# Another order of the seven products over two column blocks of the feed-forward input

## The chip, the cores and the metric

The kernel runs on one core of a Trainium2 chip, in one launch. The time is the device time of that launch in microseconds; a comparison takes runs of both kernels on the same chip. Besides the times there is one execution with the hardware profiler on, from which all rows below come.

## What is computed

Two layers of an encoder on 512 tokens of width 1024. Each layer has a mixing part (four kinds of heads, an output projection) and a feed-forward part; only the latter is touched. Cut to that part, the reference reads:

```python
h = rmsnorm(x, ffn_norm_pre[l])
gate, up = jnp.split(h @ ffn_w_in[l], 2, axis=-1)      # 2 x 2816 columns
f = (jax.nn.silu(gate) * up) @ ffn_w_out[l]
x = x + rmsnorm(f, ffn_norm_post[l])
```

The 2816 columns of `gate` and of `up` are 22 blocks of 128 each (`KF`).

## The kernel before

Every matrix is held as two float32r parts, a high one and the remainder, and a product of two matrices is three matmuls (high by high, high by low, low by high), issued by `mm3`. ScalarE makes the high part with a copy that the profile calls CAST, VectorE the low part with a subtraction (TENSOR_TENSOR into a `wl` or `m` tile).

In the feed-forward input the first three blocks (`NP`) of each layer are multiplied plainly. For the blocks 3 to 21, here called pairs (gate and up of one block over two halves of the rows of h, 256 tokens each, and two halves of the inner dimension), the 2 by 2 block product is formed with seven products in place of eight. A product is 12 matmuls of 256 columns over four tiles of 128 (`prod`, L1466) and adds into one half of a PSUM bank. Each pair has two banks: `bd`, with the halves u0 and g1, and `bx`, with g0 and u1. Products and halves: 1 into g0; 5 into u1; 6, 7 and 4 into u0; 3 into g1; 2 into g0.

Between the products the other engines work on the same two banks (`pair_side`, L1480):

- after 1: ScalarE copies g0 (in bx) to u0 (in bd). The profile calls it COPY bd<-bx.
- after 5: ScalarE copies u1 out of bx, COPY m<-bx.
- after 6: VectorE adds that copy to u0 and writes g1 (TENSOR_TENSOR bd<-bd,m).
- after 7: VectorE adds it to u0 again, into SBUF; this is the up half u1 (TENSOR_TENSOR m<-bd,m).
- after 2 and after 3: ScalarE's Silu of g0 and of g1 (ACTIVATE m<-bx, m<-bd); after 3 and after 4: VectorE's products of gate and up.

`ffn_in` (L1528) issues the products of two neighbouring pairs interleaved: of the new pair, and of the old one before it. The list of tuples at L1549 sets the order; the last entry of a tuple names a piece of the side work that must have been issued before.

The program has no order written out by hand for the whole. `go` (L350) runs generators ("threads") against modelled clocks and issues, each time, the instruction that it believes can start first; a `yield "P"`, `"A"`, `"V"`, `"G"`, `"D"` gives up the turn until an instruction of TensorE, ScalarE, VectorE, GpSimd or a transfer is due. `prod` yields once per two of its four tiles, so that a product can be issued in two halves of six matmuls. What is issued runs in that order on each engine. Where two engines touch one PSUM bank, the built program has a semaphore wait between them, whichever half of the bank each uses.

The weights of a pair are four tiles, of which two are formed by sums: `pair_load` (L466) loads a, e, c, b, d with SyncE and adds into e and c with GpSimd's accumulating transfers (L513); `form` (L546) splits one of them into the two parts, in the order of the consumption, which `i`, the running number of a weight, enforces; `sums` (L521) makes a2 = a + e and b2 = b + a2 on VectorE. In the numbers of the products: a is for 1, e for 5, a2 for 6, b for 2, c for 7, d for 4, b2 for 3. `w_load` (L441) hands out the numbers. Tiles come from a pool of 74 (`m`) and from four pairs of `wh` and `wl`.

Of the kernel before, what the change touches and what calls it, by code (L numbers as in the profile page):

```python
# [11 lines left out]
AF = mybir.ActivationFunctionType  # L12
# [4 lines left out]
L = 512  # L17
# [4 lines left out]
KF = FF // P  # L22
# [6 lines left out]
NP = 3  # L29
# [10 lines left out]
HALF = 256  # L40
# [196 lines left out]
class Builder:  # L237
# [203 lines left out]
    def w_load(self):  # L441
        n = 0
        for src, kind in self.stream():
            if kind == "pair":
                yield from self.pair_load(*src, n)
                n += 7 if src[1] > NP else 5
                n += 2 if src[1] == KF - 1 else 0
                continue
            yield lambda: self.tok["s"] or len(self.tok["m"]) >= 2 + STAGE
            k = "s" if self.tok["s"] else "m"  # L450
            self.take(k, 1 if k == "s" else 2)
            yield "D"
            if k == "s":
                st = self.wsp.tile([P, 1024], F32, tag="ws", name=self.nm("ws"))
                self.dma(st, src, 524288)
                half = [st[:, h * 512:(h + 1) * 512] for h in range(2)]
            else:
                half = [self.m(), self.m()]
                for h in range(2):
                    self.dma(half[h], src[:, h * 512:(h + 1) * 512], 262144)  # L460
            for h in range(2):
                self.spawn(self.w_split(n + h, half[h], kind, "" if k == "s" and h == 0 else k),
                           1 if n > 5 else n // 2 - 2.5)
            n += 2

    def pair_load(self, l, i, n):  # L466


        w = self.d["wf1"]
        src = {"a": w[l, i, 0][:, 0:512], "b": w[l, i, 0][:, 512:1024], "c": w[l, i, 1][:, 0:512],  # L470
               "d": w[l, i, 1][:, 512:1024]}
        q = {"n": set()}
        self.pairs[l, i] = q
        prev = self.pairs.get((l, i - 1))
        yield lambda: l in self.room_ok and i - self.pnow < 4
        order = (("a", "a", None), ("e", "c", "d"), ("c", "a", "c"), ("b", "b", None), ("d", "d", None))
        if SUMS == "V":
            order = (("a", "a", None), ("c", "c", None), ("d", "d", None), ("b", "b", None), ("e", None, None))

        late = i > NP  # L480
        at = dict(zip(("a", "e", "a2", "b", "c"), (n, n + 1, n + 2 + late, n + 3 + 2 * late, n + 4 + 2 * late)))
        for x in ("a", "e"):
            self.spawn(self.form(at[x], q, x), 1)
        if late:
            self.spawn(self.form(n + 2, prev, "d"), 1)
        self.spawn(self.form(at["a2"], q, "a2"), 1)
        if late:
            self.spawn(self.form(n + 4, prev, "b2"), 1)
        for x in ("b", "c"):
            self.spawn(self.form(at[x], q, x), 1)  # L490
        if i == KF - 1:
            for j, x in enumerate(("d", "b2")):
                self.spawn(self.form(n + 7 + j, q, x), 1)
        self.spawn(self.sums(q), 1)
        for name, first, more in order:
            yield lambda: len(self.tok["m"]) >= 1 + ROOM
            self.take("m", 1)
            q[name] = self.m()
            if first:
                self.spawn(self.part_load(q, name, src[first], src[more] if more else None), 0)  # L500
# [976 lines left out]
                     skip_group_check=True)  # L1477
        self.give(*w[2:])

    def pair_side(self, b, q, f, i):  # L1480

        u0, g1, g0, u1 = b[0][:, 0:HALF], b[0][:, HALF:L], b[1][:, 0:HALF], b[1][:, HALF:L]
        yield lambda: 1 in q
        yield "A"
        self.act.copy(u0, g0)
        q.add("u0")
        yield from self.need(2, 0)
        e, a = self.m(), self.m()
        yield lambda: 5 in q
        yield "A"  # L1490
        self.act.copy(e[:, 0:HALF], u1)
        yield lambda: 6 in q
        yield "V"
        self.dve.tensor_tensor(g1, u0, e[:, 0:HALF], ALU.add)
        q.add("g1")
        yield lambda: 7 in q
        yield "V"
        self.dve.tensor_tensor(e[:, HALF:L], u0, e[:, 0:HALF], ALU.add)
        q.add("u1")
        yield lambda: 2 in q  # L1500
        yield "A:Silu"
        self.act.activation(a[:, 0:HALF], g0, AF.Silu)
        self.give("x")
        yield lambda: 3 in q
        yield "A:Silu"
        self.act.activation(a[:, HALF:L], g1, AF.Silu)
        yield "V"
        self.dve.tensor_tensor(a[:, HALF:L], a[:, HALF:L], e[:, HALF:L], ALU.mult)
        self.give("m")
        yield lambda: 4 in q  # L1510
        yield "V"
        self.dve.tensor_tensor(a[:, 0:HALF], a[:, 0:HALF], u0, ALU.mult)
        self.give("d")
        self.spawn(self.f_conv(i, a, f), 4)
# [13 lines left out]
    def ffn_in(self, l, h, ok, f):  # L1528
        def done(i, b):
            if i % 2:  # L1530
                self.spawn(self.ffn_act(i // 2, b[i - 1:i + 1], f), 2)

        hf = {}
        self.conv, self.pnow = False, NP
        self.spawn(self.h_forms(l, h, ok, hf), 2)
        yield from self.parts(h, ok, "dx" * NP, CUTS, done)
        yield lambda: all((n, 3) in hf for n in (4, 7))
        self.give("m", 4)
        old = None
        for i in range(NP, KF + 1):  # L1540
            new = None
            if i < KF:
                self.pnow = i
                b = []
                for n in "dx":
                    b.append((yield from self.acq(n)))
                new = (b[1][:, 0:HALF], b[0][:, HALF:L], b[0][:, 0:HALF], b[1][:, HALF:L], set())
                self.spawn(self.pair_side(b, new[4], f, i), 0)
            for who, n, at, wait in ((new, 1, 0, 0), (new, 5, 3, 0), (old, 4, 2, "u1"), (new, 6, 2, "u0"),  # L1549
                                     (old, 3, 1, "g1"), (new, 2, 0, 0), (new, 7, 2, "g1")):  # L1550
                if who:
                    if wait:
                        yield lambda: wait in who[4]
                    yield from self.prod(who[at], n, hf, n == 1)
                    who[4].add(n)
            old = new
        self.conv = True
        self.give("m", 28)
# [153 lines left out]
```

## Time and profile before

| | us |
|---|---|
| median of 3 runs (1276.7 to 1277.62) | 1277.46 |
| profiled execution, its own time | 1276.97 |
| its span, first to last instruction | 1275.2 |
| TensorE busy in the span | 1225.8 (96%) |
| VectorE busy | 787.8 (62%) |
| ScalarE busy | 657.4 (52%) |
| pairs of layer 0, about | 309 to 514 |
| pairs of layer 1, about | 940 to 1146 |

The span is what the page divides; 1.8 us of the profiled execution lie around it. Busy TensorE is not TensorE at its peak, since matmuls overlap; the starts of the matmuls tell the pace.

### The profile page before, as it was taken

The page shows a single profiled execution, that of the slowest core. Times are in us where ns is not written, and L with a number is a line of the kernel's source. Part 1 is how long each engine was busy: PE and PEld are TensorE (multiplying, and loading weights), DVE is VectorE, ACT ScalarE, POOL GpSimd, SP SyncE. Part 2 cuts the span into 40 slices and gives each one's busy share as a digit, 9 for nine tenths or more (in the row PEclk, how much of TensorE's full clock was granted, in tenths as well). Part 3 has the DMA queues.
Part 4 walks back from the last instruction along what each step waited for, and adds up shares of the span by engine and source line. Part 5 has one row for each costly group of instructions (what it writes and reads, how often), then busy time and mean ns, then how long its engine had stood idle before and what let it go on. Part 6 is the DMA issues. An engine that isn't in the chain of part 4 may idle for free.

```text
span 1275.2 us, 21195 instructions
## 1 busy us (share of the span) xinstructions
PE 1225.8 (96%) x7906; PEld 1068.0 (84%) x7906; DVE 787.8 (62%) x1602; ACT 657.4 (52%) x1448; POOL 227.1 (18%) x216
## 2 busy tenths in 40 slices
PE   7999999999999999999999899999999999999997
PEld 7876777789999999888887676778899999998886
DVE  6477665589666777612555767655886667766222
ACT  6476744665444555523548656554654445545230
POOL 5021111241111110202230111112311111102120
PEclk9999999999999999999999899999999999999999
DMA  6532224127667552325451221250566665513331
GB/s 222 182 99 84 67 72 169 42 83 184 157 173 176 141 139 83 100 99 165 146 198 50 67 84 43 100 189 1 124 172 168 180 168 133 135 58 123 108 116 67
DMA packets 77239, 155.11 MB, mean 122 GB/s; under 512 B 9040, under 2 KB 9424, under 8 KB 77136
## 3 DMA queue, kind: packets, MB, share of 16 engines
q1 hardware_dynamic: 65904, 133.31, 32.1%
q0 software_dynamic: 10944, 19.93, 9.5%
q8 instruction: 62, 1.02, 0.3%
q10 hardware_dynamic: 288, 0.52, 0.2%
q14 instruction: 41, 0.34, 0.1%
HBM read 147.44 MB, written 4.19 MB: 119 GB/s over the span
## 4 chain that ended last, share of the span: by engine, by line
PE 83%; ACT 6%; DVE 6%; issue 2%; POOL 1%; DMA 1%; SPq 0%; DVEq 0%; POOLq 0%; ACTq 0%
PE bx L191 42%; PE bd L191 41%; DVE m L191 5%; ACT m L191 4%; ACT bd L191 1%; POOL s L191 1%; ACT L191 1%; ACT wh L191 1%; DVE s L191 1%; DMA ws<-in_w 0%; POOL wl L191 0%; DMA m<-in_w 0%; PE warm L191 0%; DVE wl L191 0%; POOL m L191 0%
## 5 line engine op out<-in xcount | busy, mean ns | idle before, releaser
L191 PE MATMUL bd<-m,wh 128*128 128x256 f32 (+1 forms) x1648 | 364.6, 316 | 1.3 <-ACT wh L191 1.2
L191 DVE TENSOR_TENSOR wl<-m,wh 128x512 fp32r<-128x512 f32 x284 | 197.1, 694 | 179.6 <-ACT wh L191 162.8
L191 ACT CAST wh<-m 128x512 fp32r<-128x512 f32 x316 | 195.8, 619 | 191.6 <-PE bd L191 112.8
L191 PEld LDWEIGHTS bd<-m,wh 128*128 128x128 f32 x1648 | 267.2, 191 | 22.7 <-issue 6.0
L191 PE MATMUL bx<-m,m 128*128 128x256 f32 (+8 forms) x1688 | 249.3, 337 | 11.3 <-DVE m L191 9.0
L191 PE MATMUL bd<-m,wl 128*128 128x256 f32 (+1 forms) x824 | 257.5, 313 | 0.0
L191 PEld LDWEIGHTS bx<-m,m 128*128 128x128 f32 (+3 forms) x1688 | 188.9, 177 | 61.8 <-issue 26.4
L191 DVE TENSOR_TENSOR m<-m,m 128x512 f32<-128x512 f32 (+3 forms) x288 | 172.2, 623 | 26.2 <-ACT m L191 23.8
L191 PE MATMUL bx<-m,wh 128*128 128x256 f32 x864 | 163.3, 287 | 15.2 <-ACT bd L191 15.2
L191 PEld LDWEIGHTS bd<-m,wl 128*128 128x128 f32 x824 | 157.1, 191 | 9.4
L191 PE MATMUL bx<-wh,m 128*128 128x512 f32 x472 | 163.5, 392 | 0.0
L191 PEld LDWEIGHTS bx<-m,wh 128*128 128x128 f32 x864 | 134.1, 191 | 22.1 <-ACT bd L191 22.1
L191 PE MATMUL bd<-wh,m 128*128 128x512 f32 x360 | 128.8, 392 | 0.0
L513 POOL DMA_DIRECT2D m<-in_wf x76 | 66.6, 936 | 336.9 <-DMA m<-in_wf 130.7
L191 PE MATMUL bx<-m,wl 128*128 128x256 f32 x432 | 122.0, 282 | 0.0
L191 ACT CAST wh<-ws 128x512 fp32r<-128x512 f32 x86 | 53.2, 621 | 126.7 <-PE bd L191 77.6
L191 DVE TENSOR_TENSOR wl<-ws,wh 128x512 fp32r<-128x512 f32 x56 | 40.6, 726 | 122.3 <-ACT wh L191 122.1
L191 PEld LDWEIGHTS bx<-wh,m 128*128 128x128 f32 x472 | 89.1, 189 | 19.0 <-issue 0.5
L191 PE MATMUL bd<-m,m 128*128 128x256 f32 (+1 forms) x696 | 101.9, 300 | 0.0
L191 POOL TENSOR_TENSOR wl<-m,wh 128x512 fp32r<-128x512 f32 x32 | 48.6, 1518 | 289.3 <-ACT wh L191 231.8
L191 PEld LDWEIGHTS bd<-m,m 128*128 128x128 f32 x696 | 93.9, 194 | 3.7
L191 PE MATMUL bx<-wl,m 128*128 128x512 f32 x236 | 92.2, 391 | 0.0
(105 smaller groups left out, 1443.5 us busy)
## 6 DMA issues: line engine op xcount, KB each, us to landing
m<-in_wf SPq DMA_DIRECT2D x234, 256.0 KB, 3.5
m<-in_wf POOLq DMA_DIRECT2D x76, 256.0 KB, 4.9
ws<-in_wf SPq DMA_DIRECT2D x34, 512.0 KB, 3.7
m<-in_w SPq DMA_DIRECT2D x64, 256.0 KB, 4.4
ws<-in_w SPq DMA_DIRECT2D x16, 512.0 KB, 3.8
m<-in_wo SPq DMA_DIRECT2D x24, 256.0 KB, 4.0
m<-in_x SPq DMA_DIRECT2D x14, 256.0 KB, 3.5
m<-in_rpb SPq DMA_DIRECT2D x12, 256.0 KB, 5.2
```

Source lines behind the costliest of these rows:

```text
L191: return f(out, *a, **k)
L513: self.nc.gpsimd.dma_start(q[name], src, accum_op=ALU.add)
```

## The change

Three places are edited. The list in `ffn_in` now interleaves the products as 1 (new), 7 (old), 5 (new), 3 (old), 6 (new), 2 (new), 4 (old), where it was 1, 5 (new), 4 (old), 6 (new), 3 (old), 2, 7 (new). The side work of a pair, one generator before, is two: `pair_first` with the two copies and the Silu of g0, and `pair_sums` with the rest; they meet in `q["e"]` and `q["s0"]`. And the numbers of the weights in `w_load` and `pair_load` follow the new order, so that c, b2 and d of a pair are formed one pair later.

```diff
@@ pair_load
-        late = i > NP
-        at = dict(zip(("a", "e", "a2", "b", "c"), (n, n + 1, n + 2 + late, n + 3 + 2 * late, n + 4 + 2 * late)))
...
+        use = [(q, "a"), (prev, "c"), (q, "e"), (prev, "b2"), (q, "a2"), (q, "b"), (prev, "d")]
+        if not late:
+            use = [u for u in use if u[0] is q]
         if i == KF - 1:
...
+            use += [(q, "c"), (q, "b2"), (q, "d")]
+        for j, (o, x) in enumerate(use):
+            self.spawn(self.form(n + j, o, x), 1)
@@ pair_side, now pair_first and pair_sums
-    def pair_side(self, b, q, f, i):
+    def pair_first(self, b, q, t):
...
         yield "A"
         self.act.copy(u0, g0)
         q.add("u0")
         yield from self.need(2, 0)
-        e, a = self.m(), self.m()
+        e, a = t["e"], t["a"] = self.m(), self.m()
         yield lambda: 5 in q
         yield "A"
         self.act.copy(e[:, 0:HALF], u1)
+        q.add("e")
...
+    def pair_sums(self, b, q, t, f, i):
...
+        yield lambda: 6 in q and "e" in q
@@ ffn_in
-            for who, n, at, wait in ((new, 1, 0, 0), (new, 5, 3, 0), (old, 4, 2, "u1"), (new, 6, 2, "u0"),
-                                     (old, 3, 1, "g1"), (new, 2, 0, 0), (new, 7, 2, "g1")):
+            for who, n, at, wait in ((new, 1, 0, 0), (old, 7, 2, "g1"), (new, 5, 3, 0), (old, 3, 1, "g1"),
+                                     (new, 6, 2, "u0"), (new, 2, 0, 0), (old, 4, 2, "u1")):
```

**TensorE, from product 1 to product 5 of one pair.** In these rows `bx` and `bd` are the banks (the number is that of a pair's tile), the first operand is a part of h, the second a part of the weight. Before, in layer 0, the end of product 1 and most of product 5:

```order
L191 MATMUL bx_4635<-m_2484,wh_4582 128x256 x2
L191 MATMUL bx_4635<-m_2484,wl_4583 128x256
L191 MATMUL bx_4635<-m_3285,wh_4598 128x256 [waits Activation_49]
L191 MATMUL bx_4635<-m_3285,wh_4598 128x256
L191 MATMUL bx_4635<-m_3285,wl_4599 128x256 [waits DVE_49]
L191 MATMUL bx_4635<-m_3287,wh_4598 128x256 x2
L191 MATMUL bx_4635<-m_3287,wl_4599 128x256
L191 MATMUL bx_4635<-m_3392,wh_4598 128x256 [waits Activation_49]
L191 MATMUL bx_4635<-m_3392,wh_4598 128x256
L191 MATMUL bx_4635<-m_3392,wl_4599 128x256
```

The same place in the change: first the end of product 1 and the start of product 7 of the old pair, then its end and the start of product 5 of the new one:

```order
L191 MATMUL bx_4757<-m_2484,wh_4703 128x256 x2
L191 MATMUL bx_4757<-m_2484,wl_4704 128x256
L191 MATMUL bd_4618<-m_3311,wh_4721 128x256 [waits DVE_49,Activation_49]
L191 MATMUL bd_4618<-m_3311,wh_4721 128x256
L191 MATMUL bd_4618<-m_3311,wl_4722 128x256 [waits DVE_49]
```

```order
L191 MATMUL bd_4618<-m_3541,wh_4721 128x256 x2
L191 MATMUL bd_4618<-m_3541,wl_4722 128x256
L191 MATMUL bx_4757<-m_3285,wh_4739 128x256 [waits Activation_49]
L191 MATMUL bx_4757<-m_3285,wh_4739 128x256
L191 MATMUL bx_4757<-m_3285,wl_4740 128x256 [waits DVE_49]
```

Before, product 5 followed product 1 into the same bank, six of its matmuls were issued ahead of the copy of g0, and the seventh waits for ScalarE. Now the 12 matmuls of product 7 into another bank stand between, and product 5 waits at its first matmul.

**VectorE, around the add of u1 after product 7** (`m` from `bd` and `m`). Before, then now:

```order
L191 TENSOR_TENSOR wl_4875<-m_4503,wh_4874 128x512 [waits PE_49,Activation_49]
L191 TENSOR_TENSOR m_4674<-m_4674,bd_4634 128x256
L191 TENSOR_TENSOR wl_4893<-m_4431,wh_4892 128x512 [waits DMAHW3_49,PE_49,Activation_49]
L191 TENSOR_TENSOR m_4810<-bd_4772,m_4810 128x256 [waits PE_49]
L191 TENSOR_TENSOR wl_4915<-m_4502,wh_4914 128x512 [waits Activation_49]
```

```order
L191 TENSOR_TENSOR wl_4878<-m_4483,wh_4877 128x512 [waits PE_49,Activation_49]
L191 TENSOR_TENSOR m_4657<-m_4657,bd_4618 128x256 [waits PE_49]
L191 TENSOR_TENSOR wl_4898<-m_4351,wh_4897 128x512 [waits Activation_49]
L191 TENSOR_TENSOR wl_4918<-m_4482,wh_4917 128x512 [waits PE_49,Activation_49]
L191 TENSOR_TENSOR m_4793<-bd_4756,m_4793 128x256 [waits PE_49]
```

The add now has the low part of a2 (`wl_4918`) ahead of it. On ScalarE, from the copy of g0 to the Silu of g1, the order before and now is:

```order
L191 COPY bd_4772<-bx_4773 128x256 [waits PE_49]
L191 CAST wh_4798<-m_4233 128x512 [waits Activation_49]
L191 COPY m_4810<-bx_4773 128x256 [waits DVE_49,PE_49]
L191 CAST wh_4819<-m_4380 128x512 [waits DMAHW2_49,DVE_49]
L191 CAST wh_4836<-m_4369 128x512 [waits DMASW3_49,DVE_49,PE_49]
L191 CAST wh_4855<-m_4502 128x512 [waits DMAHW4_49,DVE_49,PE_49]
L191 ACTIVATE m_4674<-bd_4634 128x256 [waits PE_49]
```

```order
L191 COPY bd_4756<-bx_4757 128x256 [waits PE_49]
L191 CAST wh_4780<-m_4348 128x512 [waits DVE_49,Activation_49]
L191 CAST wh_4802<-m_4351 128x512 [waits DMAHW2_49,DVE_49,PE_49]
L191 COPY m_4793<-bx_4757 128x256 [waits PE_49]
L191 CAST wh_4819<-m_4249 128x512 [waits DMAHW6_49,DVE_49]
L191 ACTIVATE m_4657<-bd_4618 128x256 [waits DVE_49,PE_49]
```

One CAST stands between the two copies before, two now; the Silu of g1 now waits for VectorE as well (for the add of u1, which reads the same bank).

**TensorE, the last pair of a layer, which no new pair follows.** Before, the end of product 7 and the start of product 4; then the change, from the middle of product 3 to that of product 4:

```order
L191 MATMUL bd_5994<-m_3541,wh_6037 128x256 x2
L191 MATMUL bd_5994<-m_3541,wl_6038 128x256
L191 MATMUL bd_5994<-m_3332,wh_6055 128x256 [waits DVE_49,Activation_49]
L191 MATMUL bd_5994<-m_3332,wh_6055 128x256
L191 MATMUL bd_5994<-m_3332,wl_6056 128x256
```

```order
L191 MATMUL bd_5978<-m_2489,wl_6056 128x256
L191 MATMUL bd_5978<-m_2491,wh_6055 128x256 [waits DVE_49]
L191 MATMUL bd_5978<-m_2491,wh_6055 128x256
L191 MATMUL bd_5978<-m_2491,wl_6056 128x256
L191 MATMUL bd_5978<-m_2493,wh_6055 128x256 x2
L191 MATMUL bd_5978<-m_2493,wl_6056 128x256
L191 MATMUL bd_5978<-m_3332,m_6067 128x256 [waits Activation_49]
L191 MATMUL bd_5978<-m_3332,m_6067 128x256
L191 MATMUL bd_5978<-m_3332,m_6068 128x256
L191 MATMUL bd_5978<-m_3334,m_6067 128x256 x2
L191 MATMUL bd_5978<-m_3334,m_6068 128x256
L191 MATMUL bd_5978<-m_3447,m_6067 128x256 [waits Activation_49]
```

Before, the products 4 and 3 stood behind the last 7 and only the first of them waited for VectorE. Now 7, 3 and 4 of the last pair stand one behind the other in one bank, 3 waits in its middle for VectorE (the add of u1) and 4 in its middle for ScalarE (the Silu of g1).

## Rows read from the trace of the kernel before

**Rows 1.** The page: busy time by engine, and the chain that ended last.

```profile
PE 1225.8 (96%) x7906; PEld 1068.0 (84%) x7906; DVE 787.8 (62%) x1602; ACT 657.4 (52%) x1448; POOL 227.1 (18%) x216
...
PE 83%; ACT 6%; DVE 6%; issue 2%; POOL 1%; DMA 1%; SPq 0%; DVEq 0%; POOLq 0%; ACTq 0%
```

**Rows 2.** Waits of TensorE: total us, times, longest; whole span, then 309 to 514.

```profile
PE bx L191 <- ACT bd L191: 16.9, 38, 0.4
...
PE bx L191 <- ACT bd L191: 8.5, 19, 0.4
```

**Rows 3.** Chain of waits in one pair of layer 0: start, us, what.

```profile
471.24 2.17 PE bx L191 x18
...
473.43 0.37 ACT bd L191
...
473.84 0.98 PE bx L191 x6
474.82 4.32 PE bd L191 x36
479.14 1.44 PE bx L191 x12
480.58 1.44 PE bd L191 x12
482.02 2.17 PE bx L191 x18
```

**Rows 4.** Timeline behind the next pair's start, on TensorE, ScalarE and VectorE.

```profile
483.89 0.28 PE L191 MATMUL bx<-m,wl 128*128 128x256 f32 x1
484.21 0.36 ACT L191 COPY bd<-bx 128x256 f32<-128x256 f32 x1 [1.32 <-PE bx L191]
484.48 0.62 ACT L191 CAST wh<-m 128x512 fp32r<-128x512 f32 x1
484.62 0.50 PE L191 MATMUL bx<-m,wh 128*128 128x256 f32 x2 [0.45 <-ACT bd L191]
...
484.96 0.28 PE L191 MATMUL bx<-m,wl 128*128 128x256 f32 x1
...
485.13 0.69 DVE L191 TENSOR_TENSOR wl<-m,wh 128x512 fp32r<-128x512 f32 x1 [1.81 <-ACT wh L191]
```

**Rows 5.** Windows, the pairs of layer 0 in two stretches (engines' busy us, clock, DMA share, GB/s).

```profile
323.36:410.00 86.64, 83.07 (x678) 81.46 (x677) 55.99 (x99) 41.03 (x85) 13.87 (x16) 1.00 0.70 173
410.00:513.00 103.00, 98.99 (x809) 97.16 (x808) 73.21 (x126) 52.24 (x106) 10.36 (x12) 1.00 0.45 116
```

**Rows 6.** Chain of waits at the first pair of layer 0, between products 1 and 5.

```profile
314.61 0.37 ACT bd L191
```

**Rows 7.** Groups by form, 323.7 to 506.96: busy us, mean ns; idle before, released by.

```profile
L191 DVE TENSOR_TENSOR wl<-m,wh 128x512 fp32r<-128x512 f32 x102 | 70.5, 691 | 44.7 <-ACT wh L191 40.3
L191 ACT CAST wh<-m 128x512 fp32r<-128x512 f32 x102 | 63.2, 620 | 41.1 <-PE bd L191 32.3 <-PE bx L191 4.7 <-ACT m L191 2.1
...
L191 DVE TENSOR_TENSOR m<-bd,m 128x256 f32<-128x256 f32 x17 | 7.2, 424 | 4.0 <-PE bd L191 4.0
...
L191 ACT ACTIVATE m<-bd 128x256 f32<-128x256 f32 x17 | 6.5, 384 | 17.2 <-PE bd L191 17.2
```

**Rows 8.** Transfers of the feed-forward weights by queue: count, KB, us to landing.

```profile
m<-in_wf SPq DMA_DIRECT2D x234, 256.0 KB, 3.5
m<-in_wf POOLq DMA_DIRECT2D x76, 256.0 KB, 4.9
```

**Rows 9.** Timeline at the last pair of layer 0: TensorE, ScalarE, VectorE.

```profile
514.07 0.28 PE L191 MATMUL bd<-m,wl 128*128 128x256 f32 x1
514.96 0.47 PE L191 MATMUL bd<-m,wh 128*128 128x256 f32 x2 [0.61 <-ACT wh L191]
...
514.27 0.62 ACT L191 CAST wh<-ws 128x512 fp32r<-128x512 f32 x1 [0.78 <-PE bd L191]
...
514.39 0.42 DVE L191 TENSOR_TENSOR m<-bd,m 128x256 f32<-128x256 f32 x1 [1.70 <-PE bd L191]
```

More of the change, by code (lines that the diff above doesn't have):

```diff
@@ L445, in w_load @@
                 yield from self.pair_load(*src, n)
-                n += 7 if src[1] > NP else 5
-                n += 2 if src[1] == KF - 1 else 0
+                n += (7 if src[1] > NP else 4) + (3 if src[1] == KF - 1 else 0)
                 continue
@@ L480, in pair_load @@
         late = i > NP
-        at = dict(zip(("a", "e", "a2", "b", "c"), (n, n + 1, n + 2 + late, n + 3 + 2 * late, n + 4 + 2 * late)))
[L482 to L490, printed above, removed]
+        use = [(q, "a"), (prev, "c"), (q, "e"), (prev, "b2"), (q, "a2"), (q, "b"), (prev, "d")]
+        if not late:
+            use = [u for u in use if u[0] is q]
         if i == KF - 1:
-            for j, x in enumerate(("d", "b2")):
-                self.spawn(self.form(n + 7 + j, q, x), 1)
+            use += [(q, "c"), (q, "b2"), (q, "d")]
+        for j, (o, x) in enumerate(use):
+            self.spawn(self.form(n + j, o, x), 1)
         self.spawn(self.sums(q), 1)
@@ L1478, in prod @@
         self.give(*w[2:])
-    def pair_side(self, b, q, f, i):
-        u0, g1, g0, u1 = b[0][:, 0:HALF], b[0][:, HALF:L], b[1][:, 0:HALF], b[1][:, HALF:L]
+    def pair_first(self, b, q, t):
+        u0, g0, u1 = b[0][:, 0:HALF], b[1][:, 0:HALF], b[1][:, HALF:L]
         yield lambda: 1 in q
@@ L1491, in pair_side @@
         self.act.copy(e[:, 0:HALF], u1)
-        yield lambda: 6 in q
+        q.add("e")
+        yield lambda: 2 in q
+        yield "A:Silu"
+        self.act.activation(a[:, 0:HALF], g0, AF.Silu)
+        self.give("x")
+        q.add("s0")
+    def pair_sums(self, b, q, t, f, i):
+        u0, g1 = b[0][:, 0:HALF], b[0][:, HALF:L]
+        yield lambda: 6 in q and "e" in q
+        e, a = t["e"], t["a"]
         yield "V"
@@ L1499, in pair_side @@
         q.add("u1")
[L1500 to L1503, printed above, removed]
         yield lambda: 3 in q
@@ L1509, in pair_side @@
         self.give("m")
-        yield lambda: 4 in q
+        yield lambda: 4 in q and "s0" in q
         yield "V"
@@ L1547, in ffn_in @@
                 new = (b[1][:, 0:HALF], b[0][:, HALF:L], b[0][:, 0:HALF], b[1][:, HALF:L], set())
-                self.spawn(self.pair_side(b, new[4], f, i), 0)
-            for who, n, at, wait in ((new, 1, 0, 0), (new, 5, 3, 0), (old, 4, 2, "u1"), (new, 6, 2, "u0"),
-                                     (old, 3, 1, "g1"), (new, 2, 0, 0), (new, 7, 2, "g1")):
+                t = {}
+                self.spawn(self.pair_first(b, new[4], t), 0)
+                self.spawn(self.pair_sums(b, new[4], t, f, i), 0)
+            for who, n, at, wait in ((new, 1, 0, 0), (old, 7, 2, "g1"), (new, 5, 3, 0), (old, 3, 1, "g1"),
+                                     (new, 6, 2, "u0"), (new, 2, 0, 0), (old, 4, 2, "u1")):
                 if who:
```

## The prediction

> **What bounds the kernel now.** I began with the page. TensorE is busy 96% of the span, and the chain that ended last runs on it for 83% [rows 1]. So time can only come out of TensorE's own work or of its waits. Next I read TensorE's waits. One of them is regular: matmuls into bx wait for ScalarE's write of bd, 38 times in the span, 19 of them in the stretch of layer 0 that holds the pairs [rows 2]. There are 19 pairs in a layer, so this is one wait per pair: product 5 behind the copy of g0 to u0.
>
> The chain of waits shows its price. From one pair's product 2 to the next the chain takes 482.02 - 471.24 = 10.78 us, and it holds 18 matmuls, the copy, then 6, 36, 12 and 12: 84 in all, seven products [rows 3]. The 36 in one run take 4.32 us, 0.12 us each, and a product of 12 takes 1.44. 84 x 0.12 = 10.08. The wait therefore costs 10.78 - 10.08 = 0.70 us in every pair. The timeline gives the same piece by piece: the last matmul ahead of the wait starts at 483.89, so the next could start at 484.01; the copy starts when the matmuls have drained, at 484.21, takes 0.36, and TensorE resumes at 484.62 [rows 4]. That is 0.61 us late. The two matmuls then take 0.34 where two take 0.24 otherwise, which is the other 0.10.
>
> The two products touch different halves of the bank, so only the bank makes them wait for the copy. The clock is no part of it: it stands at 1.00 (the level of 2.4 GHz) in both stretches of the pairs, all these gaps included [rows 5].
>
> **What the change does to a pair.** In the new order the old pair's product 7 stands between 1 and 5. Its 1.44 us cover the wait if the copy is done in them: product 5 could start at 484.01 + 1.44 = 485.45 on the clock of [rows 4], and the copy ends at 484.57. That leaves 0.88 us, and even a CAST of 0.62 in front of the copy [rows 7] would fit. The wait goes in 18 of the 19 pairs of each layer. The first pair has no old one, so its product 5 follows 1 as before and its wait [rows 6] stays. 36 x 0.70 = **25.2 us** less. The gap alone would be 36 x 0.61 = 22.0; I take 0.70, since it is the difference of whole periods.
>
> **What is late next.** Each of the other waits of the new order must be looked at in the same way. Product 3 (old) now waits for VectorE's add of u1, which needs product 7, one product earlier. On VectorE this add has the low part of a2 ahead of it, and that waits for a CAST that ScalarE does right behind the copy. All of this chain can be read in [rows 4], since before the change the same CAST and split follow the copy: the CAST starts at 484.48 and the split of 0.69 at 485.13, so it ends at 485.82. Product 7 has ended earlier, at about 485.45 + 0.16 = 485.61. The add takes 0.42 [rows 7], ends at about 486.24, and TensorE would hear of it 0.05 later, at 486.29. Product 3 is due at 484.01 + 2.88 = 486.89. The spare is 0.60 us. This is the tightest place of the new order. The others (6, 2, 7 and 4 on the work behind them) have two or three products, 2.9 us or more, between; nothing for them.
>
> The engines have room. Per pair ScalarE does 7 CASTs of 0.62, two copies of 0.37 and two Silus of 0.38, 5.8 us; VectorE 7 splits and 2 sums of 0.69 and four half-width operations of 0.42, 7.9 us. Both stay under 10.08, VectorE at 78%. The split of the side work into two pieces adds no instruction.
>
> Weights: c, b2 and d are formed up to one pair later, so their buffers come free later and the loads that reuse them start later. A load takes 3.5 us on SyncE's queue and 4.9 on GpSimd's, which adds into a loaded tile [rows 8], together 8.4. By the order of instructions, the last matmul that a load waits for stands at least 205 matmuls ahead of the first that needs its data (235 before), 24.6 us at 0.12. The cover is three times the need: nothing, and if it were gone, see the second rival.
>
> **The end of each layer's pairs.** Before, product 4 of the last pair waits behind 7: the last matmul starts at 514.07, the next could at 514.19 and does at 514.96, 0.77 late, plus 0.07 at restart, 0.84 in all; VectorE's add (514.39 to 514.81) and a CAST (to 514.89) end about together in it [rows 9]. Now 7, 3 and 4 stand in one bank, and 3 waits in its middle for the add, 4 in its middle for the Silu of g1. By the price of the copy, plus what these take longer than its 0.36: 0.76 for the add and 0.72 for the Silu (0.42 and 0.38), 1.48. So each layer pays 1.48 - 0.84 = 0.64 more, **1.3 us** for both. Bounds: nothing for either wait (1.7 less), or a split of 0.69 and a CAST of 0.62 in front of them (3.9 more).
>
> **The sum.** -25.2 + 1.3 = -23.9. Against the profiled execution, 1276.97 - 23.9 = 1253.1; its time is 0.5 below the median of the runs, from which it would be 1253.6. I say **1253.3 us**. All that follows the pairs runs on TensorE and moves up by the same amount. With the bounds above this case reaches from about 1250 to 1256.5.
>
> **The rivals.**
>
> *The add of u1 comes late by one operation.* If a second split of 0.69 gets ahead of it, it is 0.09 beyond its spare of 0.60, and with 0.10 at restart product 3 loses 0.19 in each pair: 36 x 0.19 = 6.8, 1260.1 us. For it: it is the tightest place, and VectorE is busy 71% of the second stretch [rows 5]. Against it: the order has one split there and VectorE waits 40.3 us for CASTs in this stretch [rows 7], so nothing queues up in front of it. 9%.
>
> *The loads become the bound.* In the first eight pairs of a layer the transfers run at 173 GB/s at a share of 0.70 [rows 5], and a period of 10.08 wants 185. If they cannot, these pairs keep their period: 16 x 0.70 = 11.2, 1264.5 us. Against it: the share would only go to 0.75, and no load stands among what ended the idle time before the CASTs [rows 7]. 5%.
>
> *Slower: VectorE takes over as the brake.* ScalarE's Silu of g1 now stands behind VectorE's add of u1, in the same bank, and the next pair's CASTs stand behind that Silu, the splits behind the CASTs. Lateness of the add would so return to VectorE. With two splits more ahead of it (1.38), product 3 waits 1.38 - 0.60 + 0.10 = 0.88 per pair, more than the 0.70 removed: 36 x 0.18 + 1.3 = 7.8 more, 1285 us. It decides once the add is later than 1.20 us beyond today's chain. The trace of before speaks against it by the same idle time of VectorE. 5%. The Trainium skill, "PSUM — Partial Sum Buffer", section "PSUM bank collisions raise a hardware error", says that any two of TensorE, ScalarE and VectorE have to be kept apart by bank and quadrant and not by address, reads against reads too. By that rule the Silu and the add must be serialised though they use different halves; the trace of before agrees for TensorE against ScalarE (the 0.70 us), and for ScalarE against VectorE no row of it shows a price.
>
> *The wait only moves.* If the add is late by just those 1.20 us, product 3 pays the 0.70 that product 5 paid, and the change buys nothing but its end: 1278.3 to 1278.8 us. Or the change would not do what it says, with product 5 still next to 1; the built order excludes that. 4%.
>
> **The numbers.** The forecast has 77%. The range of 1250 to 1262 holds it and the first rival, 86% together, less what may fall outside of their own bounds. About 0.2%, 2.6 us, is what a measurement of this kernel can tell from no change. Faster by more: the forecast and the first two rivals, 91%. Within it: the wait that only moves, 4%. Slower: 5%.
>
> **What would show it.** In the profile after, TensorE's wait of bx for ScalarE's bd should be there twice, not 38 times; the chain of a pair should hold no ScalarE piece and have a period of 10.08 us. At the end of each layer's pairs there should be two waits of about 0.7 us, one for VectorE and one for ScalarE. The 18 remaining periods at 10.27 with waits of bd for VectorE would be the first rival, at 10.78 in the first eight alone the second, above 10.78 the slower case. I am wrong if TensorE's waits in the pairs sum to more than some 6 us over both layers.

## The result, and the profile after

The change takes 1256.02 us (median of 4 runs, 1254.46 to 1256.65) against 1277.54 before on the same chip: a ratio of 0.9827, 95% interval 0.981 to 0.9844. A second set of five runs gave 0.9822 (0.9809 to 0.9836). The forecast was 1253.3 us, the range 1250 to 1262. The profiled execution took 1254.46, its span 1252.7.

TensorE's waits in the kernel after, total us, times and longest:

```profile
PE bx L191 <- DVE m L191: 22.5, 18, 4.8
...
PE bd L191 <- DVE m L191: 1.0, 2, 0.5
PE bd L191 <- ACT m L191: 0.9, 2, 0.5
PE bx L191 <- ACT bd L191: 0.9, 2, 0.4
```

Of the 38 waits of bx for ScalarE's copy [rows 2] two are left, one for the first pair of each layer. New are two waits for VectorE and two for ScalarE: the ends of the two layers' pairs. The chain of waits of the kernel after, from the third-last pair of layer 0 to the start of its output product (start, us, what):

```profile
484.44 2.88 PE bd L191 x24
487.32 1.44 PE bx L191 x12
488.76 1.44 PE bd L191 x12
490.20 1.44 PE bx L191 x12
491.64 1.44 PE bd L191 x12
493.08 1.44 PE bx L191 x12
494.52 2.88 PE bd L191 x24
...
498.84 3.61 PE bd L191 x30
...
502.47 0.43 DVE m L191
...
502.95 1.71 PE bd L191 x12
...
504.69 0.39 ACT m L191
...
505.12 0.97 PE bd L191 x6
506.10 2.06 PE bx L191 x9
```

A pair is now seven products without a gap, 494.52 - 484.44 = 10.08 us, where it was 10.78 [rows 3]. At the end of the layer's pairs stand the two waits, for the add of u1 and for the Silu of g1; the 48 matmuls from 498.84 on take 506.10 - 498.84 = 7.26 us, 1.50 more than 48 x 0.12. The tightest place of the new order, in the timeline of the kernel after:

```profile
441.28 0.36 ACT L191 COPY bd<-bx 128x256 f32<-128x256 f32 x1 [0.94 <-PE bx L191]
...
441.55 0.62 ACT L191 CAST wh<-m 128x512 fp32r<-128x512 f32 x1
...
442.20 0.69 DVE L191 TENSOR_TENSOR wl<-m,wh 128x512 fp32r<-128x512 f32 x1 [1.14 <-ACT wh L191]
...
442.81 0.42 DVE L191 TENSOR_TENSOR m<-bd,m 128x256 f32<-128x256 f32 x1
...
443.96 0.40 PE L191 MATMUL bd<-m,wh 128*128 128x256 f32 x2
```

Copy, CAST, split and add stand one behind the other as the prediction took them from the trace of before [rows 4]. The add ends at 443.23 and product 3 starts on time, at 443.96, 0.73 later; less the 0.05 that passes before TensorE hears of it, the spare is 0.68 us.

Where the time went, by the starts of the same work in both chains (first pair of a layer, first piece of its output product):

| stretch | before | after | difference |
|---|---|---|---|
| start to the first pair of layer 0 | 309.54 | 309.50 | -0.04 |
| pairs of layer 0 | 208.52 | 196.60 | -11.92 |
| output product of layer 0, mixing of layer 1, to its first pair | 422.44 | 423.83 | +1.39 |
| pairs of layer 1 | 208.53 | 196.60 | -11.93 |
| the rest | 126.17 | 126.17 | 0.00 |

The pairs gain 23.85 us, where the prediction's sum was 23.9. The profiled execution is only 22.5 faster, since 1.39 us come back in one stretch, where the change moves nothing. Most of it comes at the gap of TensorE between the two layers. The windows of before, then of the kernel after, start both times with the same VectorE operation in the gap; the second window is the run of 72 matmuls behind it (us; busy us of TensorE, its weight loads, VectorE, ScalarE, GpSimd; granted clock; DMA share; GB/s):

```profile
647.36:654.64 7.28, 4.13 (x24) 3.93 (x23) 6.34 (x11) 2.47 (x9) 3.06 (x5) 0.78 0.87 277
654.64:663.43 8.79, 8.79 (x74) 8.79 (x74) 0.48 (x2) 0.00 (x0) 0.00 (x0) 0.99 0.72 256
```

```profile
635.39:643.31 7.92, 4.77 (x24) 4.57 (x23) 6.52 (x12) 2.47 (x9) 3.06 (x5) 0.66 0.93 290
643.31:652.60 9.29, 9.29 (x74) 9.29 (x74) 0.29 (x1) 0.00 (x0) 0.00 (x0) 0.93 0.59 213
```

TensorE idles 3.15 us in the gap both times (7.28 - 4.13 and 7.92 - 4.77). The same matmuls then run at a mean granted clock of 0.66 and 0.93, after 0.78 and 0.99: a larger part of the time falls at the lower of the clock's two levels, 1.2 GHz in place of 2.4. The two windows take 16.07 and 17.21 us, 1.14 of the 1.39. About 0.3 more come some 65 us later, where the same 89 matmuls take 12.12 us after 11.83, at 0.80 after 0.82.

### The profile page after: what moved, and what is told of

The parts are those of the page before. It is cut to its first block, busy times and chain, and to the rows that moved or that the text cites. A ratio compares the mean times of both kernels' runs of the same rounds, so it can differ in the third digit from the quotient of the medians.

```text
span 1252.7 us, 21225 instructions
## 1 busy us (share of the span) xinstructions
PE 1218.5 (97%) x7906; PEld 1067.7 (85%) x7906; DVE 783.7 (63%) x1602; ACT 658.2 (53%) x1448; POOL 232.6 (19%) x216
## 4 chain that ended last, share of the span: by engine, by line
PE 84%; DVE 6%; ACT 5%; issue 2%; POOL 1%; DMA 1%; SPq 0%; POOLq 0%; DVEq 0%; ACTq 0%
PE bx L191 42%; PE bd L191 41%; DVE m L191 5%; ACT m L191 4%; POOL s L191 1%; ACT L191 1%; DVE s L191 1%; DMA ws<-in_w 0%; ACT wh L191 0%; POOL wl L191 0%; POOL m L191 0%; DMA m<-in_w 0%; PE warm L191 0%; DVE wl L191 0%; DVE sbd L191 0%
## 5 line engine op out<-in xcount | busy, mean ns | idle before, releaser
L191 PE MATMUL bd<-m,wh 128*128 128x256 f32 (+1 forms) x1696 | 374.5, 315 | 1.1 <-DVE m L191 1.0
L191 PEld LDWEIGHTS bd<-m,wh 128*128 128x128 f32 x1696 | 275.0, 191 | 22.6 <-issue 6.0
L191 PE MATMUL bx<-m,m 128*128 128x256 f32 (+8 forms) x1736 | 255.8, 335 | 9.5 <-DVE m L191 9.0
L191 PE MATMUL bd<-m,wl 128*128 128x256 f32 (+1 forms) x848 | 264.3, 312 | 0.0
L191 PEld LDWEIGHTS bx<-m,m 128*128 128x128 f32 (+3 forms) x1736 | 195.5, 178 | 59.2 <-issue 26.0
L191 PEld LDWEIGHTS bd<-m,wl 128*128 128x128 f32 x848 | 161.8, 191 | 9.3
L191 PE MATMUL bx<-m,wh 128*128 128x256 f32 x832 | 154.3, 283 | 0.9 <-ACT bd L191 0.9
L191 PE MATMUL bx<-m,wl 128*128 128x256 f32 x416 | 117.7, 283 | 0.0
L191 POOL TENSOR_TENSOR wl<-ws,wh 128x512 fp32r<-128x512 f32 x30 | 47.9, 1596 | 263.9 <-ACT wh L191 242.8
L191 PE MATMUL bd<-m,m 128*128 128x256 f32 (+1 forms) x624 | 92.4, 303 | 0.9 <-ACT m L191 0.9
```

The costliest lines, as they stand in the source:

```text
L191: return f(out, *a, **k)
```

## The experiments

The theory: product 5 waited for the copy of g0 because both use one bank, and product 7 between them covers that wait. Rivals: the two pieces of the side work do it; ScalarE's pace or the flow of data was the brake; for the 1.39 us that come back, that denser pairs lower the clock.

**The order without the two pieces.** The new list and the new numbers of the weights, with the old `pair_side`.

```diff
-                t = {}
-                self.spawn(self.pair_first(b, new[4], t), 0)
-                self.spawn(self.pair_sums(b, new[4], t, f, i), 0)
+                self.spawn(self.pair_side(b, new[4], f, i), 0)
```

> The new order of the products, with the two banks' side work in one piece as before. Theory (the gain is the 0.70 us wait of product 5 for the copy of g0, covered by product 7): TensorE's waits of bx for ScalarE's bd are 2, the period of a pair is 10.08 us, and the time is that of the change, 1254 to 1257 us. Rival (the gain comes from the side work in two pieces): 38 waits, period 10.78, 1277 us.

Measured: 1255.34 us, ratio 0.9818 (0.9798 to 0.9839), two waits of bx for ScalarE's bd. The pieces are not needed for the gain.

**The two pieces without the order.** The old list with `pair_first` and `pair_sums`, the reverse of the diff above.

> The old order of the products, with the side work in two pieces. Theory: nothing changes, 38 waits of bx for ScalarE's bd, period 10.78 us, 1276 to 1279 us. Rival (the two pieces do it): period 10.08, about 1255 us.

Measured: 1277.39 us, ratio 1.0 (0.999 to 1.0009), 38 waits, 17.0 us of them. The pieces alone bring nothing.

**A bank of its own for product 5.** The kernel before, with a third bank per pair.

```diff
-        u0, g1, g0, u1 = b[0][:, 0:HALF], b[0][:, HALF:L], b[1][:, 0:HALF], b[1][:, HALF:L]
+        u0, g1, g0, u1 = b[0][:, 0:HALF], b[0][:, HALF:L], b[1][:, 0:HALF], b[2][:, 0:HALF]
...
         self.act.copy(e[:, 0:HALF], u1)
+        self.give("x")
...
-                for n in "dx":
+                for n in "dxx":
...
-                    yield from self.prod(who[at], n, hf, n == 1)
+                    yield from self.prod(who[at], n, hf, n in (1, 5))
```

> The old order and one piece, but product 5 goes into a PSUM bank of its own, so that it shares none with the copy of g0. Theory (it is the shared bank that makes product 5 wait, not the data and not ScalarE's pace): all 38 waits go, 38 x 0.70 = 26.6 us, the period of a pair is 10.08 with product 5 right behind product 1, and the time is 1251 us, up to 1.5 more if the clock at the change of layers falls as in the run of the change. Rival (ScalarE or the data flow is the brake, and the order relieves it): period stays 10.78, 1277 us.

Measured: 1251.19 us, ratio 0.9793 (0.9777 to 0.981), and no wait of bx for ScalarE's bd is left. The chain of this kernel over one pair, and its timeline at the copy of g0:

```profile
400.20 2.88 PE bx L191 x24
403.08 4.32 PE bd L191 x36
...
410.28 2.88 PE bx L191 x24
```

```profile
401.67 0.36 ACT L191 COPY bd<-bx 128x256 f32<-128x256 f32 x1 [0.61 <-PE bx L191]
401.71 0.28 PE L191 MATMUL bx<-m,wl 128*128 128x256 f32 x1
```

Product 5 follows product 1 at once (the 24 matmuls in one run), the copy runs beside it, and the pair takes 410.28 - 400.20 = 10.08 us. So neither the data nor ScalarE's pace made product 5 wait, but the shared bank.

**Product 5 beside 1 again.** The change with 5 and 7 swapped, and with them 3 and 6, so that 7 and 3 stay apart; the weights' numbers likewise.

```diff
...
-            for who, n, at, wait in ((new, 1, 0, 0), (old, 7, 2, "g1"), (new, 5, 3, 0), (old, 3, 1, "g1"),
-                                     (new, 6, 2, "u0"), (new, 2, 0, 0), (old, 4, 2, "u1")):
+            for who, n, at, wait in ((new, 1, 0, 0), (new, 5, 3, 0), (old, 7, 2, "g1"), (new, 6, 2, "u0"),
+                                     (old, 3, 1, "g1"), (new, 2, 0, 0), (old, 4, 2, "u1")):
```

> The change with products 5 and 7 swapped, so that 5 stands next to 1 again and nothing else does: 1, 5, 7 (old), 6, 3 (old), 2, 4 (old). Theory: 38 waits of bx for ScalarE's bd, period 10.78 us, and with the 0.64 us per layer at the end of the pairs that the change also has, 1277.5 + 1.3 = 1279 us (1278 to 1280.5). Rival (another part of the new order or the two pieces make the gain): about 1256 us.

Measured: 1278.15 us, ratio 1.0005 (0.9995 to 1.0014). 38 waits are back, 17.1 us of them. In the chain of this kernel two neighbouring copies stand 417.98 - 407.20 = 10.78 us apart:

```profile
407.20 0.36 ACT bd L191
...
417.98 0.36 ACT bd L191
```

**Product 3 beside 7.** The same neighbourhood in the other bank: 1, 7 (old), 3 (old), 5, 6, 2, 4 (old); the weights' numbers likewise.

```diff
...
-            for who, n, at, wait in ((new, 1, 0, 0), (old, 7, 2, "g1"), (new, 5, 3, 0), (old, 3, 1, "g1"),
+            for who, n, at, wait in ((new, 1, 0, 0), (old, 7, 2, "g1"), (old, 3, 1, "g1"), (new, 5, 3, 0),
```

> The change with products 3 (old) and 5 (new) swapped: 1, 7 (old), 3 (old), 5, 6, 2, 4 (old). Product 3 stands next to 7 in the old pair's bank, with VectorE's add of u1 between. Theory (each such neighbourhood costs one drain, one operation and one restart, whichever engine it is): 36 more waits of bd for VectorE at 0.76 us, period 10.84, the change's 1256 + 27.4 = 1283 us (1281 to 1286). Rival (only ScalarE's copy within bx matters; an add by VectorE is hidden): 1256 us.

Measured: 1282.41 us, ratio 1.0036 (1.0018 to 1.0054): 0.4% slower than before. 38 waits of bd for VectorE's m. In this kernel's chain VectorE's pieces of two neighbouring pairs start at 400.97 and 411.81:

```profile
400.97 0.44 DVE m L191
...
401.45 0.98 PE bd L191 x6
...
411.81 0.43 DVE m L191
```

That is 10.84 us, 0.76 over 10.08, the price that the prediction had made for this wait from the copy's (0.70, and 0.06 for the longer operation). A neighbour in the same bank costs the like, whether ScalarE or VectorE stands between.

**One and two more operations ahead of the add of u1.**

```diff
         yield lambda: 7 in q
         yield "V"
+        for _ in range(1):    # 2 in the second kernel
+            self.dve.tensor_tensor(self.scr, self.scr, self.scr, ALU.mult)
         self.dve.tensor_tensor(e[:, HALF:L], u0, e[:, 0:HALF], ALU.add)
...
```

> The change with one more VectorE operation of 0.69 us (a tile of zeros by itself) right ahead of the add of u1 in every pair, to try the spare of 0.60 us that the prediction gives product 3. In the trace of the change the add ends at 443.23 and product 3 starts at 443.96. Theory: the spare is about used up, 0 to 0.19 us per pair, 0 to 7 us more than the change: 1256 to 1263 us. Rival (the waits have ample cover, the trace of the change shows no slack because VectorE works ahead): no change, 1256; rival (VectorE at 78% is near its limit): over 1265 us.

> The same with two such operations. Theory: the add is about 1.3 us later than in the change, past its spare of 0.60 to 0.70 by 0.6 to 0.8, with 0.10 at restart: 0.7 to 0.88 us per pair, 25 to 32 us more than the change, 1281 to 1288 us, so as slow as before or slower; waits of bd for VectorE, 38 of them. Rival (ample cover): 1256 us.

Measured: 1254.63 us with one (ratio 0.982, 0.9798 to 0.9841) and 1280.31 with two (1.0014, 1.0005 to 1.0023). The time with one is that of the change, and both lie a little under what had been expected (1256 to 1263, and 1281 to 1288). The timeline with one:

```profile
403.64 0.44 PE L191 MATMUL bd<-m,wh 128*128 128x256 f32 x2
...
413.21 0.42 DVE L191 TENSOR_TENSOR m<-bd,m 128x256 f32<-128x256 f32 x1
...
413.64 0.28 PE L191 MATMUL bx<-m,wl 128*128 128x256 f32 x1
413.76 0.44 PE L191 MATMUL bd<-m,wh 128*128 128x256 f32 x2
```

The add ends at 413.63. Product 3 is due 0.12 behind the matmul of 413.64 and starts on time, at 413.76; less the 0.05, some 0.08 of the spare are left. Its first two matmuls take 0.44 us where they take 0.40 in the change, and the pairs' period is 10.10 to 10.12 in place of 10.08; why these two are slower is not shown. So one operation uses up nearly all of the spare. With two, TensorE's timeline shows product 3 waiting, 10.83 us from pair to pair:

```profile
432.46 0.51 PE L191 MATMUL bd<-m,wh 128*128 128x256 f32 x2 [0.49 <-DVE m L191]
...
443.29 0.51 PE L191 MATMUL bd<-m,wh 128*128 128x256 f32 x2 [0.49 <-DVE m L191]
```

That is 0.75 per pair, inside the 0.7 to 0.88 expected, and all of the gain is gone. The waits of bd for VectorE are 34, where 38 were expected; the first pairs of a layer have room.

**The third bank, and no wait at a layer's end.** As the kernel with the third bank, and in the last pair of a layer product 7 ahead of 2, c's number ahead of b's.

```diff
...
+            end = [(new, 2, 0, 0), (new, 7, 2, "g1")]
+            if i == KF - 1:
+                end.reverse()
             for who, n, at, wait in [(new, 1, 0, 0), (new, 5, 3, 0), (old, 4, 2, "u1"), (new, 6, 2, "u0"),
                                      (old, 3, 1, "g1")] + end:
```

> The kernel with a bank of its own for product 5 and the old order, and in the last pair of a layer 7 ahead of 2, so that product 2 covers the add of u1 there too. Theory: no wait in the pairs at all; of the kernel with the third bank the 0.84 us at each layer's end go, 2 x 0.84 = 1.7 us, 1249.5 us (1248 to 1251.5 with the clock), the fastest of all here. Rival (product 4 then waits for the CAST that ended with the add before): 1251 us as without it.

Measured: 1250.81 us, ratio 0.9785 (0.9767 to 0.9802), the fastest here, though its interval overlaps that of the third bank alone. The chain of this kernel at the end of layer 0's pairs has no piece of another engine:

```profile
489.91 1.44 PE bd L191 x12
491.35 2.88 PE bx L191 x24
494.23 5.76 PE bd L191 x48
499.99 1.44 PE bx L191 x12
501.43 2.88 PE bd L191 x24
504.31 2.07 PE bx L191 x9
```

From the first pair (309.91) to the output product it takes 194.40 us, the kernel with the third bank alone 195.23 (309.48 to 504.71): the 0.83 of a layer's end are gone. The time alone does not tell this, 1251 us would have been the rival's.

**The change once more, and moved in time.** For the 1.39 us at the start of layer 1, first the change itself again.

> The change itself once more, to tell two causes of its missing 1.4 us in the profiled execution apart, lost at the start of layer 1 with the granted clock lower there. Theory (the clock of that stretch varies from one execution to the next, in this kernel as in the one before): executions at a mean granted clock of 0.994 to 0.995 are among the new ones and take 1251.5 to 1253.5 us, the prediction's 1253.3; those at 0.989 take about 1256.5. Rival (the change itself lowers the clock): all at 0.992 or less, none under 1254.

Measured: 1254.27 to 1257.06, at mean granted clocks of 0.989 to 0.992; none of the nine executions of the change ran at 0.994 or more, and the profiled one has the run of 72 matmuls at 9.29 us again. So the theory as put there, that the clock merely varies between executions, missed. That left the change itself with its denser pairs, or the moment at which the gap comes. Runs above already speak against the denser pairs: the kernel with the third bank has the same pairs of 10.08 us, and two of its four executions ran at 0.995; the new order with the old side work in one piece ran once at 0.995, in 1251.15 us. To tell them apart, all the work behind the first matmul of layer 0's first pair was moved later, by matmuls that overwrite one another and add no value. The first pairs are also issued in a slightly other order, up to about 350 us; behind that the order on all engines is the change's.

```diff
+            if fresh and k == 0 and not self.moved_by:
+                self.moved_by = True
+                for _ in range(12):    # 28 in the second kernel
+                    self.pe.matmul(dst, w[0][:, s], t[:, 0:HALF], start=True, stop=False, skip_group_check=True)
...
```

> The change with the first matmul of the first pair of layer 0 issued 12 times more (each overwrites the one before), so that all behind it is the same work 12 x 0.12 = 1.44 us later. Theory (what the clock takes at the start of layer 1 depends on the moment at which that gap of TensorE falls, which the removed 12 us have shifted): the run of 72 matmuls at the start of layer 1, 9.29 us in the change against 8.79 before, takes under 9.1 again, the stretch from the end of layer 0 to the pairs of layer 1 gets shorter than the change's 325.9 us, and so the time grows by less than the added 1.44. Rival (the change itself, with denser pairs, lowers the clock there): 9.29 and 325.9 as in the change, and the full 1.44 more, 1257 us.

> The same with 28 matmuls, 3.36 us. Theory: the length of that stretch is another one than with 1.44, not in proportion to the delay; it may be as long again as in the change. Rival as above: 325.9 and 3.36 more, 1258.9 us.

Measured: 1255.88 us (ratio 0.9821, 0.9805 to 0.9838) and 1258.27 (0.9838, 0.9822 to 0.9854). These medians do not decide: the second is near the 1258.9 of the rival. The profiled executions tell more. Both had lost some 2 us ahead of the first pair, so the gap comes 3.50 and 5.55 us later in them than in the change. The long pieces of the chains, the end of the output product of layer 0 and the first pair of layer 1, in the change, then with 12 and with 28:

```profile
604.03 10.88 PE bd L191 x48
...
929.93 5.05 PE bx L191 x42
```

```profile
607.51 10.88 PE bd L191 x48
...
932.05 5.05 PE bx L191 x42
```

```profile
609.55 10.88 PE bd L191 x48
...
932.24 5.05 PE bx L191 x42
```

From the first of these pieces to the last the change takes 929.93 - 604.03 = 325.90 us (326.04 when it ran once more), moved by 12 matmuls 324.54, by 28 only 322.69; before it was 324.49. The windows over the same work in the gap and the same run, with 12 and with 28:

```profile
638.89:646.29 7.40, 4.25 (x24) 4.05 (x23) 6.46 (x12) 2.47 (x9) 3.06 (x5) 0.77 0.83 272
646.29:654.98 8.69, 8.69 (x74) 8.69 (x74) 0.35 (x2) 0.00 (x0) 0.00 (x0) 1.00 0.69 244
```

```profile
640.94:646.86 5.92, 2.77 (x25) 2.56 (x24) 4.99 (x6) 1.84 (x8) 3.06 (x5) 1.00 0.87 263
646.86:655.50 8.64, 8.64 (x74) 8.64 (x74) 1.83 (x7) 0.64 (x3) 0.00 (x0) 1.00 0.86 295
```

TensorE idles 3.15 us in the gap each time, as in the change, but with 28 the clock stays at 1.00, the level of 2.4 GHz, and the two windows take 14.56 us where the change takes 17.21. With 3.36 us of work added ahead of the gap, 3.21 us are gone behind it. The pairs are as dense as in the change, so dense pairs alone do not lower the clock at the start of layer 1. That the moment of the gap decides fits these traces, but it is not shown: each is one execution, in others of the same two kernels the mean clock was as low as 0.989, and what differs between executions of one kernel stays open.

## Why the prediction was right, and the step that was off

- **The wait, its place and its price: right.** 38 waits became two, the period 10.78 became 10.08. The shared bank was shown as the cause by the third bank, the cover by putting 5 back beside 1.
- **The end of each layer's pairs: right.** 1.48 us were forecast for the two waits and 1.50 measured, 0.84 had been there; the pairs of a layer gain 11.92 and 11.93 us, and 18 x 0.70 - 0.64 is 11.96.
- **The spare of the add of u1: right, 0.60 forecast, 0.68 measured.** Operations of 0.69 follow each other on VectorE at 0.61, as 442.20 and 442.81 show, which the sum did not use. With the larger spare and these shorter steps the rivals were priced too high: the first, one operation more, would have cost about 0.03 us a pair and not 0.19, the slower one, two more, 0.75 and not 0.88. The slower rival's mechanism exists: with two operations more the kernel is as slow as before.
- **The loads: right.** In the pairs no TensorE wait is for a load, though the transfers run at 183 GB/s in the first eight, where 185 had been worked out. Of the weights only c moved to the next pair; b2 and d were formed with the next pair's weights before, too, and now stand one place earlier and four later among them. The window of the kernel after:

```profile
323.16:403.80 80.64, 80.64 (x674) 80.64 (x674) 56.42 (x101) 41.93 (x86) 14.00 (x16) 1.00 0.74 183
```

- **The step that failed** is the sentence "All that follows the pairs runs on TensorE and moves up by the same amount". It held from layer 1's first pair on, to 0.01 us, but not between the layers: +1.39 us in the profiled execution, nearly all of it in stretches with a lower granted clock. That is a term that the sum did not have. The median lies another 1.6 above the profiled execution's 1254.46; the executions of the change ran at clocks of 0.989 to 0.992, where the profiled one before had 0.994. The 1254.46 are 1.2 over the forecast, the median 2.7: the forecast had taken 2.6 us as what a measurement can tell from no change, but executions of the kernel before alone reach from 1276.27 to 1281.28 us in one of the sets here.
- The rule of the Trainium skill ("PSUM — Partial Sum Buffer", section "PSUM bank collisions raise a hardware error") that engines have to be kept apart by bank and quadrant, not by address, agrees with the third bank's result: the same two operations on different banks run side by side. No run here shows a price for ScalarE against VectorE.

## What to carry to other kernels

Where two products write one bank and another engine reads it between them, look at what stands between in the queue: one product of 1.44 us of another bank hid a wait of 0.70 behind ScalarE's copy and, by the run with 3 beside 7, one of 0.76 behind VectorE's add. Another bank hides the same wait without a new order, if one is free, and in the first pair of a layer too; the wait at the end of the last pair stayed until its own products were put in another order. Before a tight place is relied on, work out its spare from the chain behind it and try it with an operation or two.

## What had not been expected

- The time of an unchanged stretch differed by more than 3 us between kernels in which it starts at different moments: 325.90, 324.54 and 322.69 us for the same work, with a mean granted clock of TensorE of 0.66, 0.77 and 1.00 in the gap between the layers. A few us of a change elsewhere can be lost or won there, and a profile's clock has to be compared stretch by stretch before a difference is put down to the edit.
